# A two-layer hybrid trunk on one core: attention slots placed ahead of an evacuation, and one empty slot per eight attention units

## The chip, the cores and the metric

The kernel runs on one NeuronCore of one Trainium2 chip, in one launch. The metric is the device time of an execution in microseconds (us). All arithmetic is float32; matmul operands are cut into two float32r parts, a high and a low one, and each product is made of three matmuls.

## The reference, cut to what matters

Two groups of tokens go through the same two layers: 1024 prompt tokens and 64 sample tokens (8 sequences of 8), 1088 columns in all, with 1024 channels. The change touches layer 0 alone, whose mixer is this:

```python
proj = hn @ w_in                                  # 1024 -> 2560
a_val, a_gate, q, k, v = jnp.split(proj, [512, 1024, 1536, 2048], axis=-1)
glu = a_val * jax.nn.sigmoid(a_gate)
a = causal_depthwise_conv(concat([conv_prev, glu]), conv_w) + conv_b   # width 31
a = jax.nn.silu(layer_norm(a, ln_g, ln_b))
b = stick_breaking_attention(q, concat([k_past, k]), concat([v_past, v]), sb_bias, q_pos, k_pos)
out = concat([a, b]) @ w_out
```

The attention has 8 heads of 64 channels. For a block of 128 queries it computes

```python
z = q @ k.T * scale + bias
log_1m = where(mask, log_sigmoid(-z), 0)
after = cumsum(log_1m, reverse=True) - log_1m
wgt = exp(where(mask, log_sigmoid(z) + after, -inf))
out = wgt @ v
```

The kernel writes this with sigmoids and products: a reverse running product of sigmoid(-z) along the keys, times sigmoid(z). After the mixer each layer has a SwiGLU feed-forward network (FFN) of width 2816. k and v are outputs too, in rows of tokens, and so is the last part of the gated convolution input.

## The kernel before, in words

**Tiling.** Activations are held with channels on the partitions. The tokens are split in two groups: `GA` is columns 0 to 511, `GB` columns 512 to 1087 (512 prompt columns and the 64 sample columns), worked on as two blocks of 288. A weight tile of 1024 by 128 comes in by one DMA of 512 KB into `stage` (4 buffers, issued by SyncE's queue, L169), is split by ScalarE into its high part (L187) and by GpSimd into its low part (L189), both in `hl`. `mm3` (L238) issues the three matmuls of each product: 24 matmuls of 512 columns for a weight tile in `GA`, 48 of 288 columns in `GB`, into one `acc` tile of PSUM.

**Foreground and background.** The order of the work is the order in which the Python code issues it; each engine then takes its instructions in that order and waits on semaphores. The foreground is a row of projections. The background is a list of generators (`flow`); a call of `bg()` advances the first of them to its next `yield`. The foreground calls it at its slots: inside `block`, ahead of the third, fifth and seventh of the eight products (`slot()` at i = 2, 4, 6), and once more after the block. So a block has four slots, and a slot stands between two pieces of 12 matmuls of 288 columns in `GB`, or of 6 matmuls of 512 columns in `GA`. A generator that yields without issuing anything leaves its slot empty: TensorE then goes straight on with the next foreground piece.

**The stages of layer 0.** In this order: the input projection of `GA` (`in_proj(GA, ...)`); the input projection of `GB` (`in_proj(GB, x1, 0, bg)`), whose background is the convolution of `GA`, its layer norm, and then the attention of `GA`; the output projection and the FFN of `GA` (`run_out`, `run_ffn`), whose background is `flow_c`: the attention of `GB`, then the convolution of `GB` beside the attention of the sample tokens over the paged cache, then the layer norm of `GB`. What is left of the background is run by `drain()` when the last piece of the FFN of `GA` begins. The code as it stood before leaves the last 12 slots of that FFN with nothing to run.

**`in_proj(GB)`.** 20 blocks of 48 matmuls, in the order `EVEN`: for each of four channel groups c a value, a gate, a q and a k tile, and then four v tiles. `acc` has two buffers. After a block the code calls `flush()`, which runs what earlier blocks have put off in `post`, then `evs[i](a)`, the evacuation of this block's `acc` by VectorE (L296: times the norm factor `rr`), and then the fourth slot. What is put off in `post` is the turning of channels into output rows: for a k or v tile `rows_out` issues five TensorE transposes (four L804 into one `m` tile, one L808 into another), two ScalarE copies (L805, L809) and two DMAs (L811, L813); for a gate tile one transpose (L790), one copy and, at the end, nine DMAs. `m` is a PSUM tile with two buffers, and all transposes of the kernel go through it.

**The attention generator.** 32 units per group, (head, query block), each a chain over four engines:

- `s1(u)`: TensorE makes z from `kt`, `qa`, `qz` (L1018), ScalarE two sigmoids of z into `q` and `be` (L1023), GpSimd clears one column (L1025);
- `s2(u)`: VectorE runs two scans on `q` (L1032 on 128 columns, L1035 on the rest) and a product into `be` (L1037);
- `s3(u)`: TensorE transposes `be` in pieces of 128 into `m` (L1047), ScalarE copies them to `wt` (L1048);
- `s4(u)`: for two units at a time, TensorE multiplies by `vrow` into `o` (L1057), ScalarE copies to its place (L1060).

At each new head `operands` queues small steps for the next one: ScalarE copies (L992, L993, L997) and VectorE subtractions (L995, L998); two of them are issued per unit. `load_v` fetches `vrow` by a DMA on SyncE's queue (L1005). In `GA` a unit has 1 to 4 pieces of keys, s3 comes three units after s1, and a unit takes one slot. In `GB` it has 5 to 8 pieces, s3 comes two units after s1, and a unit takes two slots: after `s2(u - 1)` there is a `yield 1`, and s4, s3, s1 and the small steps come in the next slot. So per head s3 has eight, seven, six and five pieces in turn.

Of the kernel before, what the change touches and what calls it, by code (L numbers as in the profile page):

```python
# [46 lines left out]
GB = Grp(HALF, T, (0, 2, 288, 0))  # L47
# [10 lines left out]
def trunk_kernel(ctx, tc, x_prompt, x_sample, cache_k, cache_v, state_conformer, state_shortconv, state_pool,  # L58
# [166 lines left out]
    def w_next(live=0):  # L225
        j = wj[0]
        wj[0] += 1
        w_split(j + 3 - live)
        w_load(need(j + 6 - live))
        return hls.pop(j)  # L230
# [3 lines left out]
    def mm3(g, acc, wh, wl, x, first, last):  # L234
        for s, (w, xi) in enumerate(((wh, 0), (wh, 1), (wl, 0))):
            for b, (c0, c1) in enumerate(g.blocks):
                xs, o = (x, 0) if not isinstance(x, tuple) else (x[0], 0) if c0 < x[2] else (x[1], x[2])
                pe.matmul(acc[:, b, :c1 - c0], w, xs[:, xi, c0 - o:c1 - o],  # L238
                          start=first and s == 0, stop=last and s == 2)
# [51 lines left out]
    def norm_b(g, ps, dg):  # L291
        spread(g, ps, dg, 1.0)
# [13 lines left out]
    def flush():  # L306
        todo = post + late
        post.clear()
        late.clear()
        for f in todo:  # L310
            f()
# [4 lines left out]
    def block(g, a, h, x, ks=K0, mid=None, slot=None):  # L316
        for i, k in enumerate(ks):
            if i == 4 and mid:
                mid()
            if slot and i in (2, 4, 6):  # L320
                slot()
            mm3(g, a, h[:, 0, k], h[:, 1, k], x[k], k == ks[0], k == ks[-1])
# [344 lines left out]
    def accs():  # L667
        return accbox["p"].tile([128, len(accbox["g"].blocks), 512], F, name="acc")
# [301 lines left out]
    def attention(g):  # L970
# [3 lines left out]
        with ExitStack() as es_:  # L974
# [11 lines left out]
            def operands(h):  # L986
                hp, hh = divmod(h, 2)
                r, o = slice(hh * 64, hh * 64 + 64), slice(64 - hh * 64, 128 - hh * 64)
                k = kt_[h] = pa.tile([128, NKEY], FR, name="kt", bufs=2)
                q = qa[h] = pa.tile([128, HALF], FR, name="qa", bufs=2)  # L990
                ks, qs = kall[r, hp, 0:NKEY], qall[r, hp, g.c0:g.c0 + HALF]
                small.append(lambda: act.activation(k[r], ks, AF.Copy))  # L992
                small.append(lambda: act.activation(q[r], qs, AF.Copy))  # L993
                for c in range(0, NKEY, 512):
                    small.append(lambda c=c: dve.tensor_tensor(k[o, c:c + 512], ks[:, c:c + 512],  # L995
                                                               f32(k[r, c:c + 512]), op=OP.subtract))
                small.append(lambda: act.activation(q[o], qs, AF.Copy))  # L997
                small.append(lambda: dve.tensor_tensor(qz[hh][r], qs, f32(q[r]), op=OP.subtract))  # L998
# [28 lines left out]
            def s2(u):  # L1027
                n = 128 * (units[u][1] + 1)
                be, q = bt[u], qt.pop(u)

                e = q[:, n - 128:n][:, ::-1]
                dve.tensor_tensor_scan(e, e, ident[:, ::-1], 0.0, op0=OP.mult, op1=OP.max)  # L1032
                if n > 128:
                    e = q[:, 0:n - 128][:, ::-1]
                    dve.tensor_tensor_scan(e, e, ones[:, 0:1].to_broadcast([128, n - 128]), q[:, n - 128:n - 127],  # L1035
                                           op0=OP.mult, op1=OP.mult)
                dve.tensor_tensor(be[:, 0:n - 1], be[:, 0:n - 1], q[:, 1:n], op=OP.mult)  # L1037

            def s3(u):
                i = units[u][1]  # L1040
                be = bt.pop(u)
                w = wt[u] = pa.tile([128, i1 - u % 2, 128], F, name=f"wt{u % 2}")
                for j0 in range(0, i + 1, 4):
                    n = min(4, i + 1 - j0)
                    m = ms().rearrange("p (j n) -> p j n", j=4)
                    for j in range(n):
                        pe.transpose(m[:, j], be[:, (j0 + j) * 128:(j0 + j) * 128 + 128], ident)  # L1047
                    act.activation(w[:, j0:j0 + n], m[:, :n], AF.Copy)  # L1048

            def s4(u):  # L1050
                h, i = units[u]
                hp, hh = divmod(h, 2)
                ws = wt.pop(u - 1), wt.pop(u)
                o = op_.tile([128, 128], F, name="o2")
                for j in range(i + 2):
                    for b in range(2 if j <= i else 1):
                        pe.matmul(o[64 * b:64 * b + 64], vrow[h][:, j], ws[b][:, j], start=j == 0, stop=j == i + 1 - b)  # L1057
                for b in range(2):
                    c = (i + 1 - b) * 128
                    act.activation(qall[hh * 64:hh * 64 + 64, hp, c:c + 128], o[64 * b:64 * b + 64], AF.Copy)  # L1060
# [8 lines left out]
            for u in range(len(units) + lag + 1):  # L1069
                if 1 <= u < len(units) + 1:  # L1070
                    s2(u - 1)
                if g is GB:
                    yield 1
                if u >= lag + 2 and (u - lag) % 2 == 0:
                    s4(u - lag - 1)
                if lag <= u < len(units) + lag:
                    s3(u - lag)
                if u < len(units):
                    h, r = divmod(u, 4)
                    if r == 0 and h < 7:  # L1080
                        operands(h + 1)
                    if r == 2 and h < 7:
                        load_v(h + 1)
                    s1(u)
                for _ in range(2):
                    if small:
                        small.pop(0)()
                yield 1
# [241 lines left out]
    def in_proj(g, x, first, slot):  # L1330
        evs = [(ev_av, ev_ag, ev_q, ev_k, ev_v)[j](g, c) for j, c in EVEN]
        for i in range(first, len(evs)):
            h = w_next()
            a = accs()
            if i == first and first:
                box = {}
                block(g, a, h, x, mid=lambda: box.setdefault("d", norm_a(g, ms, D)))
                held_back = a
                continue
            elif i == first + 1 and first:  # L1340
                block(g, a, h, x)
                norm_b(g, ms, box["d"])
                evs[first](held_back)
                evs[i](a)
                for j in range(2):
                    evs[j](None, raw[j])
            else:
                rest = g is GA and i == len(evs) - 1
                block(g, a, h, x, slot=None if rest else slot)
                flush()  # L1350
                evs[i](a)
                if rest:
                    continue
            slot()

# [705 lines left out]
```

## Time and profile before

| | |
|---|---|
| median of 3 runs | 2502.1 us (2501.27 to 2504.09) |
| the profiled execution | 2503.01 us, of which the span from first to last instruction is 2501.2 us |
| TensorE (PE) busy | 2423.2 us, 97% |
| weight loads (PEld) | 2194.5 us, 88% |
| VectorE (DVE) | 1625.4 us, 65% |
| ScalarE (ACT) | 1105.2 us, 44% |
| GpSimd (POOL) | 1618.3 us, 65% |

The profile is of one execution. Busy times of matmuls are modelled and overlap, so what TensorE loses is read from its waits: the idle time before an instruction, and what ended it. "Issue" as the cause means that the profile shows no semaphore for it. A view by windows gives busy times and the granted TensorE clock (PEclk) for chosen stretches. A timeline row shows start, duration, engine, line, operation, output and inputs.

### The profile page before, as it was taken

The page shows a single profiled execution, that of the slowest core. Times are in us where ns is not written, and L with a number is a line of the kernel's source. Part 1 is how long each engine was busy: PE and PEld are TensorE (multiplying, and loading weights), DVE is VectorE, ACT ScalarE, POOL GpSimd, SP SyncE. Part 2 cuts the span into 40 slices and gives each one's busy share as a digit, 9 for nine tenths or more (in the row PEclk, how much of TensorE's full clock was granted, in tenths as well). Part 3 has the DMA queues.
Part 4 walks back from the last instruction along what each step waited for, and adds up shares of the span by engine and source line. Part 5 has one row for each costly group of instructions (what it writes and reads, how often), then busy time and mean ns, then how long its engine had stood idle before and what let it go on. Part 6 is the DMA issues. An engine that isn't in the chain of part 4 may idle for free.

```text
span 2501.2 us, 41461 instructions
## 1 busy us (share of the span) xinstructions
PE 2423.2 (97%) x15877; PEld 2194.5 (88%) x15877; DVE 1625.4 (65%) x2288; ACT 1105.2 (44%) x1877; POOL 1618.3 (65%) x1264
## 2 busy tenths in 40 slices
PE   8999999999999999999999999998999999999998
PEld 6788877788777679999999999888889988999998
DVE  3696878977777553766656533457766659666655
ACT  5535777754444343443333422244443344443333
POOL 6764334655654576788787523277888885887775
PEclk9999999999999999999999999999999999999999
DMA  7332231234565534223332311252333332233322
GB/s 225 114 110 74 76 110 51 72 103 144 175 178 174 161 91 149 68 77 91 95 93 83 119 51 43 59 148 64 92 102 102 97 98 85 85 98 115 93 85 81
DMA packets 355486, 258.32 MB, mean 103 GB/s; under 512 B 22913, under 2 KB 303617, under 8 KB 355272
## 3 DMA queue, kind: packets, MB, share of 16 engines
q1 hardware_dynamic: 355256, 255.66, 34.6%
q8 instruction: 126, 2.06, 0.3%
q14 instruction: 72, 0.59, 0.1%
q10 hardware_dynamic: 32, 0.01, 0.0%
HBM read 237.41 MB, written 18.69 MB: 102 GB/s over the span
## 4 chain that ended last, share of the span: by engine, by line
PE 72%; DVE 12%; POOL 4%; ACT 3%; issue 3%; SPq 0%; DMA 0%; DVEq 0%; ACTq 0%; POOLq 0%
PE acc L238 41%; PE acc L540 23%; POOL hl L200 2%; DVE q L1035 1%; PE o L1057 1%; DVE hb L300 1%; PE m L1159 1%; PE m L1047 1%; PE z L1182 1%; PE z L1018 1%; POOL hl L189 1%; DVE be L1037 1%; DVE sum L203 1%; DVE hid L244 1%; DVE sum L204 1%
## 5 line engine op out<-in xcount | busy, mean ns | idle before, releaser
L189 POOL TENSOR_TENSOR hl<-stage,hl 128x512 fp32r<-128x512 f32 x464 | 637.8, 1398 | 393.6 <-ACT hl L187 279.9
L238 PE MATMUL acc<-x,hl 128*128 128x512 f32 (+1 forms) x3648 | 773.2, 350 | 9.9 <-ACT hl L187 2.8
L238 PEld LDWEIGHTS acc<-x,hl 128*128 128x128 f32 x3648 | 587.4, 190 | 73.8 <-issue 5.8
L238 PE MATMUL acc<-hid,hl 128*128 128x288 f32 (+1 forms) x3096 | 545.1, 332 | 8.6 <-DVE tmp L296 4.6
L238 PEld LDWEIGHTS acc<-hid,hl 128*128 128x128 f32 x3096 | 471.0, 190 | 54.5 <-DVE tmp L296 5.1
L540 PE MATMUL acc<-x,hl 128*128 128x288 f32 (+1 forms) x2676 | 368.0, 291 | 5.8 <-POOL hl L200 3.7
L300 DVE TENSOR_TENSOR hb<-acc,hb 128x512 f32<-128x512 f32 (+1 forms) x360 | 255.6, 718 | 171.1 <-PE acc L238 169.8
L540 PEld LDWEIGHTS acc<-x,hl 128*128 128x128 f32 x2676 | 352.3, 189 | 12.0 <-POOL hl L200 7.4
L200 POOL TENSOR_TENSOR hl<-sum,hl 128x512 fp32r<-128x512 f32 x180 | 233.4, 1325 | 170.3 <-ACT hl L199 168.3
L187 ACT ACTIVATE hl<-stage 128x1024 fp32r<-128x1024 f32 x232 | 243.8, 1054 | 215.9 <-PE acc L238 149.8
L544 DVE TENSOR_TENSOR tmp<-acc,tmp 128x288 f32<-128x288 f32 (+1 forms) x420 | 174.7, 442 | 210.6 <-ACT tmp L556 106.3
L200 POOL TENSOR_TENSOR hl<-stage,hl 128x512 fp32r<-128x512 f32 x180 | 273.9, 1540 | 14.1 <-ACT hl L199 14.1
L540 PE MATMUL acc<-b,hl 128*128 128x256 f32 (+1 forms) x1548 | 217.5, 292 | 7.7 <-DVE tmp L544 5.8
L238 PE MATMUL acc<-x1t,hl 128*128 128x288 f32 x1152 | 216.3, 296 | 1.5 <-POOL hl L189 1.5
L540 PEld LDWEIGHTS acc<-b,hl 128*128 128x128 f32 x1548 | 203.3, 191 | 13.0 <-POOL hl L200 6.4
L238 PEld LDWEIGHTS acc<-x1t,hl 128*128 128x128 f32 x1152 | 195.9, 188 | 19.5 <-POOL hl L189 1.8
L199 ACT ACTIVATE hl<-sum 128x512 fp32r<-128x512 f32 x180 | 103.0, 624 | 189.6 <-DVE sum L205 169.1
L296 DVE TENSOR_TENSOR tmp<-acc,rr 128x512 f32<-128x512 f32 (+1 forms) x108 | 75.2, 710 | 135.5 <-PE acc L238 121.6
L199 ACT ACTIVATE hl<-stage 128x512 fp32r<-128x512 f32 x180 | 105.8, 619 | 69.6 <-PE acc L238 63.6
L507 POOL TENSOR_TENSOR tmp<-tmp 128x576 f32<-128x576 f32 (+1 forms) x85 | 123.6, 1454 | 9.1 <-ACT tmp L484 8.1
L244 DVE TENSOR_TENSOR hid<-tmp,hid 128x576 fp32r<-128x576 f32 (+1 forms) x66 | 78.5, 1192 | 72.0 <-ACT hid L243 72.0
L238 PE MATMUL acc<-x1a,hl 128*128 128x512 f32 x480 | 122.3, 409 | 3.0 <-POOL hl L189 1.3
(298 smaller groups left out, 3159.6 us busy)
## 6 DMA issues: line engine op xcount, KB each, us to landing
stage<-in_w_ffn_in_dram SPq DMA_DIRECT2D x176, 512.0 KB
stage<-in_w_ffn_out_dram SPq DMA_DIRECT2D x88, 512.0 KB
stage<-in_w_in_even_dram SPq DMA_DIRECT2D x40, 512.0 KB
kst<-in_cache_k_dram SPq DMA_DIRECT2D x64, 256.0 KB
vst<-in_cache_v_dram SPq DMA_DIRECT2D x56, 256.0 KB
stage<-in_w_out_even_dram SPq DMA_DIRECT2D x16, 512.0 KB
stage<-in_w_in_odd_dram SPq DMA_DIRECT2D x16, 512.0 KB
stage<-in_w_out_odd_dram SPq DMA_DIRECT2D x16, 512.0 KB
```

The costliest lines, as they stand in the source:

```text
L187: act.activation(hl[:, 0], st, AF.Copy)
L189: pool.tensor_tensor(hl[:, 1, c], st[:, c], f32(hl[:, 0, c]), op=OP.subtract)
L199: act.activation(hl[:, 0, c], x, AF.Copy)
L200: pool.tensor_tensor(hl[:, 1, c], x, f32(hl[:, 0, c]), op=OP.subtract)
L203: todo = [lambda: dve.tensor_tensor(sb, su[:, lo], su[:, hi], op=OP.add), lambda: dve.tensor_tensor(sa[:, hi], sg[:, lo], su[:, lo], op=OP ...
L238: pe.matmul(acc[:, b, :c1 - c0], w, xs[:, xi, c0 - o:c1 - o], start=first and s == 0, stop=last and s == 2)
L244: (on or dve).tensor_tensor(dst[:, 1], src, f32(dst[:, 0]), op=OP.subtract)
L296: dve.tensor_tensor(d, a, r, op=OP.mult)
L300: dve.tensor_tensor(d, a, d, op=OP.add)
L507: (dve if both and f == NF - 1 else pool).tensor_tensor(t[:, :n], t[:, :n], u[:, :n], op=OP.mult)
L540: pe.matmul(acc[:, :w2], h[:, wi, i, k], xk[:, xi], start=k == 0 and s == 0, stop=k == 3 and s == 2)
L544: dve.tensor_tensor(out, acc[:, :w2], x, op=OP.add)
```

## The change

Two edits.

- In `in_proj`, for `GB`, the block's fourth slot is taken ahead of `flush()` and `evs[i](a)` and no longer behind them. The number of slots is the same.
- In `attention`, for `GB`, every eighth unit (u = 1, 9, 17, 25, 33) yields once more between `s2(u - 1)` and the rest of the unit. So five more slots are used up, and all later background of `flow_c` comes up to five slots later; of the 12 slots without work at the end 7 are left.

```diff
@@ -1071,6 +1071,8 @@
                     s2(u - 1)
                 if g is GB:
                     yield 1
+                    if u % 8 == 1:
+                        yield 1
                 if u >= lag + 2 and (u - lag) % 2 == 0:
                     s4(u - lag - 1)
                 if lag <= u < len(units) + lag:
@@ -1347,9 +1349,11 @@
             else:
                 rest = g is GA and i == len(evs) - 1
                 block(g, a, h, x, slot=None if rest else slot)
+                if g is GB:
+                    slot()
                 flush()
                 evs[i](a)
-                if rest:
+                if rest or g is GB:
                     continue
             slot()
```

No instruction is added or removed; they change places. TensorE at the boundary between the last but one block of `in_proj(GB)` and the last, before; `tmp` is the v tile that is turned into rows, `be` the attention's weights, `z` its scores, `x` and `hl` the projection:

```order
L238 MATMUL acc<-x_7_78,hl 128x288 x6
L804 MATMUL m<-ident,tmp 128x128 x4
L808 MATMUL m<-ident,tmp 64x128
L1047 MATMUL m<-ident,be 128x128
L1018 MATMUL z_3293<-kt,qa 128x256
L1018 MATMUL z_3293<-kt,qz_2104 128x256
L238 MATMUL acc<-x_0_71,hl 128x288 x6
```

and with the change:

```order
L238 MATMUL acc<-x_7_78,hl 128x288 x6
L1047 MATMUL m<-ident,be 128x128
L1018 MATMUL z_3279<-kt,qa 128x256
L1018 MATMUL z_3279<-kt,qz_2104 128x256
L804 MATMUL m<-ident,tmp 128x128 x4
L808 MATMUL m<-ident,tmp 64x128
L238 MATMUL acc<-x_0_71,hl 128x288 x6
```

The unit's transpose and scores now come first, the five transposes for the output rows after them. ScalarE at the same boundary, before:

```order
L1023 ACTIVATE be<-z_3252,bh 128x384
L805 ACTIVATE tmp<-m 128x512
L809 ACTIVATE tmp<-m 64x128
L1048 ACTIVATE wt_3289<-m 128x128
L1023 ACTIVATE q_3296<-z_3293,bh 128x256
L1023 ACTIVATE be<-z_3293,bh 128x256
L187 ACTIVATE hl<-stage 128x1024
```

and with the change:

```order
L1023 ACTIVATE be<-z_3252,bh 128x384
L1048 ACTIVATE wt_3275<-m 128x128
L1023 ACTIVATE q_3282<-z_3279,bh 128x256
L1023 ACTIVATE be<-z_3279,bh 128x256
L805 ACTIVATE tmp<-m 128x512
L809 ACTIVATE tmp<-m 64x128
L187 ACTIVATE hl<-stage 128x1024
```

The two copies of the output rows moved behind the unit's copy and sigmoids, and still stand ahead of the split of the next weight tile. On VectorE the evacuation L296 stands behind the unit's scans in the same way, and on SyncE's queue the load of `vrow` stands ahead of the two DMAs of rows.

The second edit, on TensorE at the start of the attention of `GB`, in the first two blocks of `run_out(GA)`, before; `z_3542` are the scores of unit 0, and the next `z` are those of unit 1:

```order
L1018 MATMUL z_3542<-kt,qa 128x512
L1018 MATMUL z_3542<-kt,qz_3502 128x512
L238 MATMUL acc<-x_5_76,hl 128x512 x6
L238 MATMUL acc<-x_6_77,hl 128x512 x6
L1018 MATMUL z_3569<-kt,qa 128x448
L1018 MATMUL z_3569<-kt,qz_3502 128x448
```

and with the change:

```order
L1018 MATMUL z_3542<-kt,qa 128x512
L1018 MATMUL z_3542<-kt,qz_3502 128x512
L238 MATMUL acc<-x_5_76,hl 128x512 x6
L238 MATMUL acc<-x_6_77,hl 128x512 x6
L238 MATMUL acc<-x_7_78,hl 128x512 x6
L1018 MATMUL z_3589<-kt,qa 128x448
L1018 MATMUL z_3589<-kt,qz_3502 128x448
```

Six more matmuls of the projection stand between the two units; the same happens at units 9, 17 and 25, and after the last unit.

## The prediction

> **What bounds the kernel now.** I read the page first, then the stages by windows, then TensorE's waits in the stretches that the change touches, then the timeline at those waits.
>
> ```profile
> span 2501.2 us, 41461 instructions
> PE 2423.2 (97%) x15877; PEld 2194.5 (88%) x15877; DVE 1625.4 (65%) x2288; ACT 1105.2 (44%) x1877; POOL 1618.3 (65%) x1264
> ```
>
> TensorE is busy for 97% of the span, so a change that moves no work can win only what TensorE waits for. The average hides where that is. The next view gives busy times of each engine (with the count of instructions), then the granted clock, by stretch: the attention of `GA` inside `in_proj(GB)`, the attention of `GB` in two parts (heads 0 to 2, and heads 3 to 7 behind the seam between output projection and FFN), and the rest of the FFN of `GA`.
>
> ```profile
> core 0: us, PE busy (x) PEld busy (x) DVE busy (x) ACT busy (x) POOL busy (x), PEclk, DMA share, GB/s
> 229.50:332.30 102.80, 95.56 (x738) 86.67 (x738) 78.66 (x114) 76.86 (x174) 29.23 (x51) 0.98 0.24 66
> 344.30:411.00 66.70, 63.70 (x408) 52.67 (x408) 63.71 (x57) 53.33 (x83) 31.70 (x29) 0.97 0.27 73
> 434.20:535.00 100.80, 95.45 (x662) 78.87 (x659) 97.00 (x82) 76.71 (x121) 57.83 (x51) 1.00 0.22 63
> 545.00:938.00 393.00, 384.72 (x2076) 306.82 (x2075) 269.53 (x432) 172.83 (x334) 234.93 (x198) 1.00 0.53 157
> ```
>
> In the first row TensorE lacks 7.2 us, and VectorE (77%) and ScalarE (75%) have room. In the second and third VectorE is busy for 63.71 of 66.70 and 97.00 of 100.80 us, 96% in both, so it paces the attention of `GB`; TensorE lacks 3.0 and 5.4 us there. So the two edits meet different limits.
>
> **First edit: the slot ahead of the rows and the evacuation.** TensorE's waits from 229.5 to 332.3 (total, times, longest):
>
> ```profile
> PE m L1047 <- issue: 4.1, 5, 1.2
> PE z L1018 <- ACT qa L997: 1.8, 1, 1.8
> PE z L1018 <- ACT be L1023: 0.9, 3, 0.4
> ```
>
> The five waits of 4.1 us stand at the five block boundaries where rows of k or v are turned. The timeline of one of them:
>
> ```profile
> 317.37 0.60 PE L804 MATMUL m<-ident,tmp 128*128 128x128 f32 x4
> 317.81 0.27 PE L808 MATMUL m<-ident,tmp 128*64 128x128 f32 x1
> 318.01 0.60 ACT L805 ACTIVATE tmp<-m 128x512 f32<-128x512 f32 x1 [0.84 <-PE m L804]
> 318.70 0.30 PE L1047 MATMUL m<-ident,be 128*128 128x128 f32 x1 [0.62 <-issue]
> 319.04 0.28 ACT L1048 ACTIVATE wt<-m 128x128 f32<-128x128 f32 x1 [0.28 <-PE m L1047]
> 319.08 1.76 PE L238 MATMUL acc<-x,hl 128*128 128x288 f32 x12
> ```
>
> L804 and L808 take both `m` buffers; the unit's transpose L1047 needs one of them back, and starts 0.09 us after L805 has emptied it at 318.61. With the change the unit's transpose comes first, while both are free, and its copy L1048 of 0.28 us runs under the scores and the four L804. The second row tile then finds its buffer empty. That removes 0.62 us at three boundaries and 1.05 and 1.18 us at the other two:
>
> ```profile
> 248.58 0.30 PE L1047 MATMUL m<-ident,be 128*128 128x128 f32 x1 [1.05 <-issue]
> 294.66 0.30 PE L1047 MATMUL m<-ident,be 128*128 128x128 f32 x1 [1.18 <-issue]
> ```
>
> What is late next: at those two the scores L1018, now issued directly behind the block, need the earlier unit's sigmoid out of the single z buffer; at such places the profile already shows waits of 0.4 us (the last row of the waits above). I take 0.45 us off each of the two, and 0.6 us for the rest: 4.1 - 0.9 - 0.6 = 2.6 us. The bounds are 4.1 us (all of it) and 0, if ScalarE, in which the two copies now follow the sigmoids, hands the wait on to the next slot. Against 0 speaks the next slot's room: the copies need 0.60 + 0.26 us, and 12 matmuls of 1.76 us come before the next transpose.
>
> The same edit puts the evacuation behind the background's VectorE work, and the load of `vrow` ahead of the two row DMAs on SyncE's queue. Nobody reads those rows soon, so the DMAs cost nothing as long as the weight loads behind them run four tiles ahead. The evacuation:
>
> ```profile
> 160.98 2.34 DVE L858 SCALAR_TENSOR_TENSOR cacc<-ext,par,cacc 128x512 f32<-128x512 f32 x3
> 163.25 0.76 DVE L296 TENSOR_TENSOR tmp<-acc,rr 128x576 f32<-128x576 f32 x1
> 163.93 1.54 DVE L858 SCALAR_TENSOR_TENSOR cacc<-ext,par,cacc 128x512 f32<-128x512 f32 x2
> 156.76 12.80 PE acc L238 x96
> ```
>
> A slot of the convolution issues two steps, 1.54 us; that much later an `acc` comes free. It is wanted back a whole block later, 6.4 us (half of 12.80 us for 96 matmuls). So this costs nothing; uncovered it would be 1.54 us at each of 20 blocks. The Trainium skill, "PSUM — Partial Sum Buffer", in its closing table of what to do, says to evacuate promptly, because PSUM is tight. By that rule this edit is the wrong way round; the rows above give it a cover of 6.4 us against 1.54, and its case is the last rival.
>
> **Second edit: five empty slots.** TensorE's waits from 332.3 to 545, and the timeline of the first of them:
>
> ```profile
> PE m L1047 <- DVE be L1037: 7.6, 6, 2.7
> ...
> 349.55 1.29 DVE L300 TENSOR_TENSOR hb<-acc,hb 128x512 f32<-128x512 f32 x2
> 351.46 2.67 DVE L1035 TENSOR_TENSOR_SCAN q<-q,ones 128x768 f32<-128x768 f32 x1
> 354.24 1.90 DVE L1037 TENSOR_TENSOR be<-be,q 128x895 f32<-128x895 f32 x1
> 350.95 2.96 PE L238 MATMUL acc<-x,hl 128*128 128x512 f32 x12
> 356.29 0.95 PE L1047 MATMUL m<-ident,be 128*128 128x128 f32 x7 [2.38 <-DVE be L1037]
> 464.50 0.96 PE L1047 MATMUL m<-ident,be 128*128 128x128 f32 x7 [2.72 <-DVE be L1037]
> 508.01 0.96 PE L1047 MATMUL m<-ident,be 128*128 128x128 f32 x7 [0.65 <-DVE be L1037]
> ```
>
> The waits of over half a microsecond stand before seven pieces, that is, at the second unit of a head: VectorE has just had the longest unit and the next head's subtractions. An empty slot gives TensorE six more matmuls of 512 columns, 1.4 us (half of the row of 12 without the overlap at its end), to issue meanwhile. They fall on heads 0, 2, 4 and 6 (units 1, 9, 17, 25). VectorE's work between is the same, so its finish stays and TensorE's wait shrinks by what it has to do: 1.4 of 2.38 us in head 0, 1.4 of 2.72 in head 4, all 0.65 in head 6. In head 2 there was no wait, so nothing; the fifth slot is behind the last unit. Sum 3.4 us. The most would be four times 1.4, 5.6 us, if the lead carried over to heads 1 and 5; the least is 0, if TensorE's later scores make VectorE start later.
>
> The wait of head 0 costs more than its length. In the stretches around it and around that of head 4 (PEclk is the column of 1.00 or 0.50):
>
> ```profile
> 354.10:357.40 3.30, 1.11 (x10) 1.14 (x11) 3.16 (x3) 1.29 (x3) 3.30 (x3) 1.00 0.88 225
> 357.50:360.80 3.30, 3.30 (x10) 2.65 (x9) 3.23 (x3) 2.06 (x5) 1.60 (x3) 0.50 0.55 159
> 460.00:463.20 3.20, 1.78 (x8) 1.11 (x6) 3.09 (x4) 1.34 (x2) 0.10 (x1) 1.00 0.59 171
> 357.85 4.34 PE L238 MATMUL acc<-x,hl 128*128 128x512 f32 x12
> ```
>
> After a stretch with 1.11 us of work the clock is halved for the next, and 12 matmuls take 4.34 us and not 2.96: 1.4 us. After one with 1.78 us of work it is not. With about 1 us of wait left in head 0 this halving should go; as VectorE paces the units I count half of it, 0.7 us (bounds 0 and 1.4). The Trainium skill, "TensorE: Matmul & The Clock Gate", section on the clock gate, says that the clock falls after at least one idle window of about 3.4 us. Here it fell after a wait of 2.38 us, so that rule read literally would have no halving to win back, and the sum would be 0.7 us less.
>
> What is moved later is the rest of the background, by five slots. It has room at the end: its last piece, and the foreground behind it:
>
> ```profile
> 918.37 3.62 DVE L963 TENSOR_TENSOR hb<-hb,tmp 128x576 f32<-128x576 f32 x2
> 926.54 0.69 DVE L300 TENSOR_TENSOR hb<-acc,hb 128x512 f32<-128x512 f32 x1 [0.71 <-PE acc L238]
> 927.94 0.69 DVE L300 TENSOR_TENSOR hb<-acc,hb 128x512 f32<-128x512 f32 x1 [0.71 <-PE acc L238]
> ```
>
> A slot there takes 1.4 us (926.54 to 927.94), the background ends near 922, and by the code's count 12 slots follow; five cost 7 us of that room and no time. Without the room they would be run by `drain()` uncovered. On SyncE's queue one weight load more comes ahead of the first cache pages; they have six slots before TensorE turns them.
>
> **Sum.** 2.6 + 3.4 + 0.7 = 6.7 us. The profiled execution took 2503.01 us, so 2496.3; it lies 0.9 us above the median of the runs, 2502.1, which gives 2495.4 us.
>
> **The rivals.**
>
> *Only the first edit pays.* VectorE at 96% leaves TensorE nothing to win: lead gained at head 0 is given back as VectorE waits for the later scores. For it: 96%; against: TensorE waits for VectorE there, and not the other way. 2502.1 - 2.6 = 2499.5 us. Chance 0.18.
>
> *Nothing moves.* The row copies, now behind the sigmoids, make the next slot wait as long, and the second edit fails as above. Against it: the 1.76 us of cover. 2502.1, within a microsecond. Chance 0.08.
>
> *Slower: the sample attention falls badly against the FFN blocks.* Five slots are one block and one slot, so each later step meets the block's evacuations at another place. The waits now, from 545 to 965:
>
> ```profile
> PE m L1159 <- DVE kth L1163: 1.3, 3, 0.7
> ```
>
> There are 48 steps, of which three wait, 0.7 us at most. If each waited 0.3 us more, that is 14.4 us: 2495.4 + 14.4 = 2509.8 us. It decides from (6.7 + 5.0) / 48 = 0.24 us a step. Against it: a step takes three slots and a block four, so the steps pass through all places already. Chance 0.05.
>
> *Slower: the accumulators come free late.* If the evacuation slips by more than the block of 6.4 us, TensorE waits at every block: 20 times 1.54 us, 31 us, 2526 us after the rest of the gain. The rows show a quarter of that delay, so 0.03.
>
> **How the numbers follow.** 0.66 is left for the forecast, likeliest. A measurement of this kernel can tell about 0.2%, 5.0 us, from no change. The forecast's gain of 6.7 us has the bounds 0 to 4.1, 0 to 5.6 and 0 to 1.4, so up to 11.1 us; I give it 0.54 above 5.0 us and 0.12 below. Faster 0.54, same 0.12 + 0.18 + 0.08 = 0.38, slower 0.08. The range goes from 2490.5 (11.1 us and half a microsecond of spread) to 2501.0, which takes in the first rival and leaves out the slower ones and most of the second.
>
> **What would show it.** First edit: no L1047 wait at the row boundaries from 230 to 332 us, and L808 without one in its place. Second: L1047 before seven pieces waits about 1 us in heads 0 and 4, PEclk stays 1.00 after it, and the background ends some 7 us nearer to the last piece of the FFN. It is wrong if VectorE's share from 344 to 535 us falls while the stretch is as long, or if L1159 or L238 gains waits.

## The result and the profile after

The changed kernel is slower: a median of 2520.5 us in 6 runs (2519.28 to 2523.11) against 2501.7 us in 6 runs of the kernel before (2500.21 to 2504.09), a ratio of 1.0076 with the interval 1.0067 to 1.0086. The forecast, 2495.4 us, lies on the wrong side of no change, and so does the whole range, 2490.5 to 2501.0 us. The first lines of the profile after:

```profile
span 2519.1 us, 41449 instructions
PE 2428.4 (96%) x15877; PEld 2197.6 (87%) x15877; DVE 1619.9 (64%) x2288; ACT 1101.6 (44%) x1877; POOL 1614.9 (64%) x1264
```

The counts of instructions per engine are those of before. TensorE's share falls from 97% to 96%: it waits more. The next two views, by windows, show where. First the kernel before, by three stretches: from the start of the output projection to the first transpose of a cache page (this is the attention of `GB`; "the attention stretch" from here on), from there to the end of the FFN of `GA` ("the sample stretch"), and the rest. The columns are as in the prediction.

```profile
332.30:553.60 221.30, 209.48 (x1296) 170.32 (x1297) 187.82 (x171) 157.79 (x251) 116.75 (x104) 0.98 0.28 78
553.60:948.50 394.90, 385.74 (x2080) 307.40 (x2078) 277.14 (x440) 175.58 (x335) 238.93 (x197) 1.00 0.54 159
948.50:2501.20 1552.70, 1516.36 (x10578) 1446.38 (x10578) 936.10 (x1349) 588.14 (x966) 1088.86 (x793) 0.99 0.30 90
```

The same stretches after, with the attention of `GA` inside `in_proj(GB)` ahead of them:

```profile
229.50:328.30 98.80, 95.06 (x738) 87.52 (x738) 79.01 (x116) 77.38 (x176) 28.39 (x51) 0.97 0.25 71
328.30:573.10 244.80, 223.05 (x1326) 180.38 (x1326) 190.40 (x176) 158.28 (x253) 117.58 (x108) 0.95 0.26 73
573.10:967.50 394.40, 379.65 (x2049) 301.39 (x2047) 268.17 (x435) 171.81 (x333) 237.22 (x193) 1.00 0.53 158
967.50:2519.10 1551.60, 1514.89 (x10578) 1445.07 (x10578) 938.61 (x1349) 588.30 (x966) 1086.87 (x793) 0.99 0.30 90
```

Five empty slots bring 30 more foreground matmuls into the attention stretch (1296 to 1326) and take about as many out of the sample stretch. By the prediction's 1.4 us for six matmuls that is 7.0 us, which is no loss, and I take it off the one and add it to the other here and in every experiment below (TensorE's busy time in the sample stretch falls by 6.1 us, 385.74 to 379.65, so up to 0.9 us of a loss there may come from this round price):

- `in_proj(GB)`: 102.8 to 98.8 us, 4.0 us won;
- attention stretch: 244.8 - 7.0 = 237.8 for 221.3 us, 16.5 us lost;
- sample stretch: 394.4 + 7.0 = 401.4 for 394.9 us, 6.5 us lost;
- the rest: 1.1 us won. Together 17.9 us, the difference of the spans.

**What was won.** TensorE's waits from 229.5 to 328.3 after the change, and one of the boundaries at which it waited before (of TensorE, the last one with rows):

```profile
PE z L1018 <- ACT qa L997: 3.4, 1, 3.4
PE z L1018 <- ACT be L1023: 0.9, 1, 0.9
```

```profile
325.44 0.27 PE L1047 MATMUL m<-ident,be 128*128 128x128 f32 x1
325.55 0.60 PE L804 MATMUL m<-ident,tmp 128*128 128x128 f32 x4
326.14 0.30 PE L808 MATMUL m<-ident,tmp 128*64 128x128 f32 x1
```

All five waits of L1047 (4.1 us) are gone, and the waits for `be` add up to 0.9 us as before. The first row is the wait at the start of this attention, 1.8 us before. TensorE comes there 0.5 us earlier, but the norm chain delivers the operands 1.1 us later: ScalarE's L997 starts at 230.34 and not at 229.22 (at 230.24 with the first edit alone). So the stage wins 4.1 us and loses 1.1 at its start; the 4.0 us come about because a wait of 0.5 us for `qz` is gone as well and TensorE's busy time is 0.5 us shorter.

**What was lost.** TensorE's waits in the attention stretch after the change:

```profile
PE m L1047 <- DVE be L1037: 10.0, 4, 4.6
PE m L1047 <- ACT wt L1048: 4.4, 2, 2.4
PE z L1018 <- ACT be L1023: 2.1, 2, 1.0
PE acc L238 <- ACT hl L187: 1.9, 1, 1.9
PE o L1057 <- ACT wt L1048: 1.6, 2, 1.4
```

Before, only the first of these was there at a length (7.6 us in six waits) beside 1.3 us for L187; all waits of the stretch grew from 13.0 to 22.9 us. The second and the fifth row are new, and the third was 0.3 us: TensorE waits for ScalarE, which is busy for 158 of 245 us. Two rows of what ScalarE itself waits for, from 328 to 590 us, before:

```profile
ACT tmp L481 <- DVE tmp L296: 6.7, 5, 2.1
ACT tmp L254 <- DVE hb L300: 6.3, 3, 5.1
```

and after:

```profile
ACT tmp L481 <- DVE tmp L296: 26.7, 5, 6.9
ACT tmp L254 <- DVE hb L300: 16.0, 5, 7.7
```

These two are the rows for the foreground's values, and both grew. L481 is not attention. It is the sigmoid of the FFN's gate, in `ev_g`, which reads what the evacuation L296 has written; L254 is the square for the norm behind the residual sum L300, in `run_out`. Both are the foreground's, and in ScalarE's queue the attention's instructions stand behind them. The timeline of the longest of these waits, in head 4 after the change (the last column is the idle time ahead of the row and what ended it):

```profile
463.82 1.38 DVE L1032 TENSOR_TENSOR_SCAN q<-q,ident 128x128 f32<-128x128 f32 x1
465.24 1.82 DVE L1035 TENSOR_TENSOR_SCAN q<-q,ones 128x768 f32<-128x768 f32 x1
467.19 1.09 DVE L1037 TENSOR_TENSOR be<-be,q 128x895 f32<-128x895 f32 x1
468.19 0.69 DVE L296 TENSOR_TENSOR tmp<-acc,rr 128x512 f32<-128x512 f32 x1
468.91 0.63 ACT L481 ACTIVATE tmp<-tmp 128x512 f32<-128x512 f32 x1 [6.92 <-DVE tmp L296]
469.57 0.55 ACT L1060 ACTIVATE hb<-o 64x128 f32<-64x128 f32 x2
470.14 1.08 ACT L1048 ACTIVATE wt<-m 128x512 f32<-128x512 f32 x2
470.80 1.03 PE L1047 MATMUL m<-ident,be 128*128 128x128 f32 x7 [1.97 <-ACT wt L1048]
471.12 0.91 ACT L1023 ACTIVATE q<-z,bh 128x768 f32<-128x768 f32 x1
472.05 0.42 DVE L1032 TENSOR_TENSOR_SCAN q<-q,ident 128x128 f32<-128x128 f32 x1 [2.45 <-ACT q L1023]
```

and the same unit before:

```profile
460.28 0.69 DVE L296 TENSOR_TENSOR tmp<-acc,rr 128x512 f32<-128x512 f32 x1
460.89 0.41 DVE L1032 TENSOR_TENSOR_SCAN q<-q,ident 128x128 f32<-128x128 f32 x1
461.34 1.82 DVE L1035 TENSOR_TENSOR_SCAN q<-q,ones 128x768 f32<-128x768 f32 x1
```

Before, VectorE does the evacuation first and then the unit's scans; after, the scans and the product first (4.3 us) and the evacuation last. ScalarE stands at L481 for 6.92 us, with the copies L1060 and L1048 and the sigmoids L1023 of the next units behind it. So TensorE lacks `m` (1.97 us), and then VectorE, which paces this stretch, lacks `q` (2.45 us). The cause of the swap is in the counting. A unit takes two slots, the scans in the first of them; a block has four slots, the fourth behind the evacuation. An even number of slots ahead keeps the scans in the second and the fourth slot, an odd number puts them into the first and the third, and what the third slot issues on VectorE stands ahead of the block's evacuation. In the changed kernel the number is odd for heads 0 and 1 (one slot) and heads 4 and 5 (three), from the second unit of the pair on, and even for the others. So the swap explains 6.92 and 6.67 of the 26.7 us, in heads 4 and 5. Another 6.32 us stand in head 3, at 447.15, where the number is even: there the evacuation, at 446.38, stands behind a unit's scans that take 1.40 and 2.64 us in place of 0.41 and 1.82. The remaining two waits, 4.35 and 2.46 us at 559.32 and 586.50, lie behind the last unit's scans.

In head 0 no L481 stands in the way yet, and the wait that the prediction meant to shorten still grew. VectorE and TensorE after (two fences):

```profile
345.01 3.44 DVE L995 TENSOR_TENSOR kt<-kall,kt 64x512 fp32r<-64x512 f32 x2
348.48 1.40 DVE L1032 TENSOR_TENSOR_SCAN q<-q,ident 128x128 f32<-128x128 f32 x1
```

```profile
354.80 0.95 PE L1047 MATMUL m<-ident,be 128*128 128x128 f32 x7 [3.53 <-DVE be L1037]
```

and GpSimd at that time, after (first fence) and before (second fence, with the subtractions):

```profile
343.65 5.95 POOL L189 TENSOR_TENSOR hl<-stage,hl 128x512 fp32r<-128x512 f32 x4 [2.55 <-ACT hl L187]
```

```profile
348.23 1.29 DVE L995 TENSOR_TENSOR kt<-kall,kt 64x512 fp32r<-64x512 f32 x2
349.85 7.42 POOL L189 TENSOR_TENSOR hl<-stage,hl 128x512 fp32r<-128x512 f32 x4 [0.86 <-ACT hl L187]
```

Before, the two subtractions L995 end before GpSimd begins its splits, and take 1.29 us; after, they run beside them and take 3.44 us. The short scan runs beside the splits in both kernels and takes 1.40 us in place of 0.67 (0.42 at 339.91, where GpSimd does nothing). The Trainium skill, "SBUF — State Buffer", section "Who interferes with whom", says that a VectorE operation on two tensors with both inputs in SBUF contends with GpSimd's reads; the rows of the subtractions agree, 1.29 against 3.44 us.

**The clock.** Of the granted clock, the records of before show three stretches at half in the attention stretch, 10.2 us; those of after five, 23.9 us. Half of the 13.7 us more is work that took twice as long: 6.8 us, which with 9.9 us of added waits makes 16.7, near the 16.5 us.

**The sample stretch** shows the same wait. ScalarE there, before and after:

```profile
ACT tmp L481 <- DVE tmp L296: 23.5, 14, 4.6
```

```profile
ACT tmp L481 <- DVE tmp L296: 45.0, 15, 5.0
```

TensorE's waits after (8.9 us in all before, 13.6 after; 0.8 us of them the `L1159` that the prediction named, in its new place L1161):

```profile
PE m L1233 <- DVE kth L1165: 4.7, 5, 1.5
```

### The profile page after: what moved, and what is told of

The parts are those of the page before. It is cut to its first block, busy times and chain, and to the rows that moved or that the text cites. A ratio compares the mean times of both kernels' runs of the same rounds, so it can differ in the third digit from the quotient of the medians.

```text
span 2519.1 us, 41449 instructions
## 1 busy us (share of the span) xinstructions
PE 2428.4 (96%) x15877; PEld 2197.6 (87%) x15877; DVE 1619.9 (64%) x2288; ACT 1101.6 (44%) x1877; POOL 1614.9 (64%) x1264
## 4 chain that ended last, share of the span: by engine, by line
PE 74%; DVE 12%; POOL 3%; ACT 3%; issue 2%; DMA 0%; SPq 0%; DVEq 0%; ACTq 0%; POOLq 0%
PE acc L238 43%; PE acc L540 23%; POOL hl L200 2%; PE o L1057 1%; DVE q L1035 1%; DVE hb L300 1%; PE z L1018 1%; PE m L1047 1%; PE z L1184 1%; PE m L1161 1%; DVE kt L995 1%; DVE sum L203 1%; DVE be L1037 1%; PE o L1256 1%; DVE sum L204 1%
## 5 line engine op out<-in xcount | busy, mean ns | idle before, releaser
L300 DVE TENSOR_TENSOR hb<-acc,hb 128x512 f32<-128x512 f32 (+1 forms) x360 | 255.3, 718 | 171.0 <-PE acc L238 169.6
L187 ACT ACTIVATE hl<-stage 128x1024 fp32r<-128x1024 f32 x232 | 243.5, 1053 | 205.7 <-PE acc L238 144.0
L540 PEld LDWEIGHTS acc<-b,hl 128*128 128x128 f32 x1548 | 201.4, 189 | 13.6 <-ACT hl L199 6.4
L296 DVE TENSOR_TENSOR tmp<-acc,rr 128x512 f32<-128x512 f32 (+1 forms) x108 | 75.1, 709 | 121.2 <-PE acc L238 112.9
L255 POOL TENSOR_TENSOR ss<-ss,tmp 128x512 f32<-128x512 f32 (+1 forms) x69 | 105.4, 1528 | 30.1 <-ACT tmp L254 19.6
```

The source lines that it names most:

```text
L187: act.activation(hl[:, 0], st, AF.Copy)
L255: pool.tensor_tensor(ss[:, g.cs], ss[:, g.cs], t[:, :g.n], op=OP.add)
L296: dve.tensor_tensor(d, a, r, op=OP.mult)
L300: dve.tensor_tensor(d, a, d, op=OP.add)
L540: pe.matmul(acc[:, :w2], h[:, wi, i, k], xk[:, xi], start=k == 0 and s == 0, stop=k == 3 and s == 2)
```

## The experiments

The theory of the order: what counts is where a unit's or a step's slots fall in the block of four, since that sets what VectorE does ahead of the evacuation and what ScalarE has queued behind L481 and L254. The rivals: a price per slot (each empty slot costs TensorE or VectorE something wherever it falls), and the first edit as the cause (the evacuation behind the background's work). Where no other diff is shown, "the first edit" is that of the change, word for word. Each ratio, with its 95% interval, is against runs of the kernel before that were made beside it (medians 2500.99 to 2501.58 us). Attention and sample stretch are of the one profiled execution, with 1.4 us a slot taken off and added, as above; before they are 221.3 and 394.9 us.

**1. The first edit alone.** The kernel before with the change to `in_proj`.

> The first edit alone. Theory (order): the loss is all in the second edit, because an odd number of empty slots puts a unit's scans ahead of the foreground's evacuation on VectorE, and ScalarE then stands in its in-order queue at the foreground's sigmoid (L481) or square (L254) with the attention's copies behind it. The first edit then keeps the 4.0 us by which the changed kernel reached the output projection earlier: 2497.7 us. Rival (late evacuation): the evacuation behind the background's work is what costs, so this kernel is slower than before, 2505 to 2520 us.

2498.39 us, ratio 0.9987 (0.9977 to 0.9997); 221.3 and 395.5 us, and the output projection begins at 328.1 for 332.3 us. The first edit keeps its gain and disturbs nothing behind it. The rival that makes it the cause falls.

**2. The second edit alone.** The kernel before with the two lines in `attention`.

> The second edit alone. Theory (order): before plus the 22.8 us that the changed kernel lost after the input projection: 2522 to 2526 us. Rival (late evacuation): near before, 2497 to 2503 us.

2521.59 us, 1.0081 (1.0064 to 1.0098), 0.4 us under what I expected; 236.0 and 403.0 us. The whole loss, in both stretches, comes with the empty slots.

**3. One empty slot at the start.** The first edit, and one slot in place of five:

```diff
-                    if u % 8 == 1:
+                    if u == 1:
                         yield 1
```

> Both edits, but a single empty slot, at unit 1, so that all later units stand shifted by one slot. Theory (order): heads 3 to 7, all within the FFN, now have their scans right ahead of the evacuation, so ScalarE's wait at L481 is as long as in the changed kernel or longer (24 to 60 us) and the time is 2510 to 2530 us. Rival (price per empty slot): one slot costs a fifth of five, 2497.7 + 16.5 / 5 = 2501 us.

2521.72 us, 1.0079 (1.0062 to 1.0096); 236.0 and 404.4 us. One slot costs as much as five. ScalarE's waits from 328 to 590 us in this kernel:

```profile
ACT tmp L481 <- DVE tmp L296: 30.2, 6, 7.0
ACT tmp L254 <- DVE hb L300: 18.9, 5, 7.7
```

They are those of the changed kernel, a little longer. So one slot ahead of everything is enough for the loss, and the later four are not needed for it. Here every unit behind unit 1 stands one slot off, in the changed kernel those of heads 0, 1, 4 and 5 alone; why the attention stretch loses no more here is open.

**4. Two empty slots in each place.** Both edits, ten slots:

```diff
                     if u % 8 == 1:
-                        yield 1
+                        for _ in range(2):
+                            yield 1
```

> Both edits, but two empty slots at each of the five units instead of one (ten in all), so the scans stay where they were beside the evacuation of an FFN block. Theory (order): ScalarE's wait at L481 for L296 falls from 24.3 us in the changed kernel back to under 8 us from 328 to 590 us, and the time is 2490 to 2503 us; the upper end if unit 12, which now comes behind the seam between output projection and FFN, keeps its wait of 4.6 us and the halved clock. Rival (price per empty slot: VectorE, 96% busy, starts later by what TensorE puts in between): ten slots cost twice as much as five, 2497.7 + 2 x 16.5 = 2531 us.

2504.84 us, 1.0015 (1.0005 to 1.0025), 1.8 us over the upper end that I had given; 222.4 and 401.2 us. With pairs the scans keep their places, L481 waits 12.6 us and not 26.7 (I had expected under 8), and the attention stretch is back within 1.1 us. Ten slots cost the attention stretch less than one does: the rival of a price per slot falls. The sample stretch, ten slots later (two and a half blocks), still loses 6.3 us.

**5. and 6. Five and four empty slots behind the attention.** The first edit, and in `flow_c`, behind `yield from attention(GB)` (4 in the other kernel):

```diff
+        for _ in range(5):
+            yield 1
```

> The first edit, and the five empty slots all behind the attention of the second group, ahead of its convolution and the sample attention. Theory (place in the block): the attention stretch is as long as with the first edit alone (221.3 us from the output projection to the first cache transpose, and 7 us of slots more), and the stretch from there to the end of the FFN loses the 6.6 us that the changed kernel lost there, because the steps meet a block's evacuation elsewhere: 2505 us. Rival (the later stretch lost only because the attention handed it a backlog): 2498.4 us, as with the first edit alone.

> As the run with five slots behind the attention, but four: a whole block. Theory (place in the block): every later step stands in its block where it stood, so nothing is lost: 2497 to 2500 us. Rival (any shift of the later work against the FFN costs): 2503 to 2505 us.

Five: 2505.64 us, 1.0016 (1.0007 to 1.0026); 221.8 and 401.3 us. Four: 2501.28 us, 0.9997 (0.9987 to 1.0006); 223.7 and 395.6 us. The sample stretch as the windows show it, five and then four slots later:

```profile
557.70:952.00 394.30, 379.67 (x2049) 301.39 (x2047) 268.08 (x435) 171.81 (x333) 237.74 (x194) 1.00 0.52 154
```

```profile
557.60:947.60 390.00, 379.56 (x2055) 302.83 (x2053) 272.56 (x436) 173.87 (x334) 235.87 (x195) 1.00 0.53 157
```

With five slots behind an undisturbed attention the sample stretch loses the same 6.4 us, and ScalarE stands at L481 for 44.9 us in it, as in the changed kernel; with four, a whole block, it loses 0.7 us, and L481 waits 31.1 us. So the loss of the sample stretch is a second one, of its own, and a shift by a whole block does without it. The wait at L481 does not measure it by itself: the ten slots of experiment 4 have 30.7 us of it in that stretch, no more than the four here, and lose 6.3 us. The median of the four-slot kernel is 1.3 us over what I expected: its attention stretch, in which nothing was edited, took 2.4 us more than in experiment 1, with a wait for L387 of 2.6 and not 1.1 us and one more stretch at half clock. Why is open.

**7. and 8. The sigmoid put off.** In the FFN the sigmoid L481 and the product behind it go to `post` and run at the next block's `flush()`; once on the changed kernel, once on the first edit alone:

```diff
             if sig:
-                s = tmp()
-                act.activation(s[:, :n], t[:, :n], AF.Sigmoid)
-                pool.tensor_tensor(t[:, :n], t[:, :n], s[:, :n], op=OP.mult)
+                def later():
+                    s = tmp()
+                    act.activation(s[:, :n], t[:, :n], AF.Sigmoid)
+                    pool.tensor_tensor(t[:, :n], t[:, :n], s[:, :n], op=OP.mult)
+                post.append(later)
```

> The changed kernel, with the FFN's sigmoid L481 and the product behind it put off to the next flush, a block later, so that ScalarE no longer meets it before the evacuation L296 is done. Theory (ScalarE's in-order queue): the waits of TensorE for ScalarE in heads 4 and 5 (4.4 us at L1047, 2.1 us at L1018) and the halved clock behind them (two times 6.8 us, worth 6.8 us) go, the wait of 4.6 us in head 3 stays: 2507 to 2514 us. Rival (VectorE's backlog alone holds TensorE): 2518 to 2522 us.

> Control for the put-off sigmoid: the first edit alone, with L481 put off in the same way. Both theories: there the evacuation stands ahead of the scans and L481 waits little, so 2496 to 2500 us, as with the first edit alone.

On the changed kernel: 2507.23 us, 1.0019 (1.0009 to 1.0028); the two stretches, without the 7.0 us taken off and added:

```profile
329.20:566.10 236.90, 219.32 (x1325) 178.43 (x1326) 191.44 (x176) 158.74 (x253) 119.21 (x108) 0.96 0.27 76
566.10:953.90 387.80, 378.38 (x2049) 301.68 (x2048) 269.65 (x435) 172.24 (x333) 237.01 (x193) 1.00 0.54 160
```

that is 229.9 and 394.8 us. On the first edit alone: 2498.74 us, 0.9989 (0.9979 to 0.9998), as without it. With the background in the same slots, and only the sigmoid and its product a block later, the whole loss of the sample stretch is gone, and 7.9 of the 16.5 us of the attention stretch. By the medians, the five slots cost 22.1 us with the sigmoid in its place (2520.5 against 2498.4) and 8.5 us with it put off (2507.2 against 2498.7), so 13.6 us go with L481. The profiled execution of the control is a short one (2496.54 us), with stretches of 219.1 and 395.2 us; against that one the put-off leaves 10.8 us in the attention stretch and gives back 5.7. Of the 8.6 us the trace shows ScalarE's wait at L254, 16.0 us as in the changed kernel, since it was not put off; the wait in head 0 (3.53 us); and one of 4.60 us in head 3, where the change moves unit 12, with its long scans, behind the seam between output projection and FFN (4.61 us in the changed kernel). How they share it was not tried.

**9., 10. and 11. Whole blocks of empty slots.** The first edit, and four slots ahead of unit 17, where before the wait of 2.72 us was; then four at units 1 and 17 each; then four at 17 with the sigmoid put off:

```diff
+                    if u == 17:
+                        for _ in range(4):
+                            yield 1
```

> The first edit, and four empty slots (a whole block) at unit 17 alone, behind the seam between output projection and FFN and ahead of the longest wait that the first edit alone leaves (2.76 us in head 4, with a halved clock behind it). Theory (order): every scan stands beside its block's evacuation where it stood, ScalarE's wait at L481 from 328 to 590 us stays under 13 us, the wait in head 4 goes: 2494 to 2498 us. Rival (price per empty slot): four fifths of 16.5 us more than the first edit alone, 2511 us.

> As the run with four empty slots at unit 17, and four more at unit 1. Theory (order, and the seam): the wait of 2.3 us in head 0 goes too, but unit 12 with its long scans comes behind the seam, as with ten empty slots, and TensorE waits 3 to 5 us in head 3: 2495 to 2501 us. Rival (price per empty slot): 2498.4 + 8 x 3.3 = 2525 us.

> The first edit, four empty slots at unit 17, and the sigmoid L481 put off by a block. Theory (order): as without the put-off, and what ScalarE still loses at L481 goes too: 2493 to 2497 us, under both kernels. Rival (VectorE at 96% paces the attention whatever ScalarE does): 2498 to 2500 us, as with the first edit and the put-off sigmoid alone.

Four at 17: 2496.73 us, 0.9981 (0.9972 to 0.9991); 220.8 and 395.9 us; the wait of head 4 is gone.

Four at 1 and 17: 2499.75 us, 0.9990 (0.9981 to 0.9999); 222.0 and 397.6 us; the wait of head 0 falls to 0.89 us, but waits of 2.26 and 3.10 us come in at 402.15 and 442.42, and the sample stretch loses 2.7 us though it stands two whole blocks later. Four at 17 with the sigmoid put off: 2497.66 us, 0.9980 (0.9971 to 0.9989); 220.1 and 395.1 us, 0.7 us over what I expected, just under the rival's 2498, and the same as without putting off. Shifted by whole blocks, empty slots take away or shorten the wait at which they are aimed, as the prediction had meant them to, and four at 17 beats both kernels. But of the 2.72 us only half a microsecond shows in the stretch: TensorE waits 1.80 us in head 6, at 509.41, where it was 0.65 with the first edit alone, and 2.6 us for L387 where it was 1.1. The interval overlaps that of the first edit alone, so it is not shown that the four slots add anything to that edit's gain.

**12. Odd shifts late, with the sigmoid put off.** The first edit, L481 put off as in experiment 7, and one empty slot at each of units 17, 25 and 33, all behind the seam.

> The changed kernel with the put-off sigmoid, and without the empty slots at units 1 and 9: heads 0 to 3 stand as before, and the three empty slots at units 17, 25 and 33 are left. Theory (what the put-off sigmoid did not win back, 8.6 us from the output projection to the first cache transpose, lies in heads 0 to 3: the square L254 behind the evacuation L300, and unit 12 behind the seam): 2496 to 2500 us. Rival (an odd shift loses by VectorE alone, in the FFN too): 2503 to 2507 us.

2500.84 us, 1.0002 (0.9992 to 1.0011), 0.8 us over what I expected; 221.2 and 397.7 us. With L481 out of the way, the odd shift in heads 4 and 5 costs the attention nothing (6 and 7 stand two slots later, an even number), so the 8.6 us that experiment 7 left come with the slots at units 1 and 9 and lie in heads 0 to 3, where L254 and the seam are. The 2.8 us in the sample stretch, with waits of 2.33 and 1.81 us at 582.93 and 614.41, are open.

## Why the prediction was wrong, step by step

**The first edit** (2.6 us, bounds 0 to 4.1): the mechanism was right. 4.0 us came in the stage, just under the upper bound; the 0.45 us that I left at two boundaries for the scores and the 0.6 us for the rest were covered, and the later start of this attention, 1.1 us, was not in the sum. Alone, by its ratio, the edit is worth 0.13%, 0.03 to 0.23, about 3.3 us with 0.8 and 5.8 as bounds, so for the whole kernel 2.6 us was a fair size. That the late evacuation costs nothing there held: TensorE waits for no `acc` from 150 to 328.3 us. The rule of the Trainium skill, "PSUM — Partial Sum Buffer", to evacuate promptly did not bite at this place. It bit in the FFN, and by another way than PSUM: not the accumulator was missed, but the value that ScalarE was to read.

**The second edit** (3.4 us won, bounds 0 to 5.6). The step that failed is "VectorE's work between is the same, so its finish stays". I counted what VectorE has to do and not in which order against the foreground's evacuation, and I priced only TensorE's side; ScalarE's queue stood in the sum at nothing. Two things were missing. First, ScalarE's queue: an empty slot moves all units behind it by one place against the block, so the evacuation L296 fell behind 4.3 us of scans and product, and L481 held up the copies and sigmoids of the next units. Putting L481 off gives back 7.9 us here, and 13.6 of 22.1 us in the whole kernel (experiment 7). Second, durations are not fixed: in head 0 the two subtractions took 3.44 and not 1.29 us where they now run beside GpSimd's splits, so VectorE finished later and the wait went from 2.38 to 3.53 us where I had written 1.0. Nor did the lower bound "0" hold, since it was reasoned from TensorE's lead alone. What the remaining 8.6 us of the attention stretch are made of is known by place, heads 0 to 3, and not by cause. A sign of the kind that the prediction set did come: VectorE's share of the attention stretch fell, from 85 to 78%, and the stretch grew longer.

**The clock** (0.7 us won): the halving at head 0 did not go, as its wait did not, and others came: 6.8 us lost. The mechanism, waits that cost more than their length, was right and worked against the change. The reading that 1.11 us of work in a window halves the clock and 1.78 does not is no rule: before, a window with 1.72 us was followed by the halved clock too (last section).

**The shift of the later background** (no cost): the step that failed is "a step takes three slots and a block four, so the steps pass through all places already". They do, but over the whole stretch it still matters where they begin: 5 slots lost 6.4 to 6.5 us (experiment 5 and the changed kernel), 10 lost 6.3, 8 lost 2.7 and 4 lost 0.7 to 1.0. With L481 put off 5 lost nothing, but 3 lost 2.8. That the loss of five slots goes through L481 is shown by experiment 7; why a beginning off by one costs when the steps go round, and what the ten, eight and three slots lose by, is open. The room at the end of the FFN was there as predicted: the last stretch took no longer.

**The rivals.** The sample attention falling badly, priced at 14.4 us, was right in place and in sign; the loss was 6.5 us, under half of that, and TensorE's waits for it stand on other lines than L1159. The larger loss, in the attention stretch, is in no rival, because each of them asked who waits for VectorE or TensorE and none who stands in ScalarE's queue. With 0.08 the slower side had far too little: the order of L296 and the scans could be read from the order of the instructions, and the 6.7 and 6.3 us that ScalarE already waited were in the trace of before.

## What to carry to other kernels

When background work with a period runs in the slots of a foreground with a period of its own, an empty slot is a shift against that period: insert whole blocks, or an amount that keeps the background's long work off the slot ahead of the evacuation. Before costing such a shift, write down for each in-order engine which foreground instruction it will stand at and what of the background is queued behind that, also on the engines that are not busy. And take a duration from a row in which the same neighbours were running.

## What the runs showed of the hardware

The clock fell to half also after a wait shorter than the stretch by which it changes (1.97 us, ahead of the row at 470.80). The changed kernel's records, by windows around two falls and one place without:

```profile
441.50:444.90 3.40, 0.00 (x0) 0.00 (x0) 3.27 (x3) 0.00 (x0) 3.40 (x4) 1.00 0.81 211
445.00:448.30 3.30, 3.30 (x13) 3.18 (x14) 3.27 (x4) 1.15 (x2) 1.35 (x2) 0.50 0.48 153
468.80:472.20 3.40, 1.06 (x8) 0.73 (x7) 0.92 (x3) 3.23 (x7) 1.26 (x1) 1.00 0.00 0
472.30:479.00 6.70, 6.14 (x16) 4.88 (x16) 5.39 (x6) 4.95 (x8) 4.47 (x5) 0.50 0.02 4
```

```profile
523.50:526.80 3.30, 1.62 (x10) 1.08 (x9) 3.20 (x3) 0.78 (x2) 0.10 (x1) 1.00 0.50 159
526.90:530.20 3.30, 3.30 (x20) 2.84 (x18) 3.23 (x4) 3.06 (x5) 0.10 (x1) 1.00 0.03 7
```

and in the kernel before:

```profile
415.50:418.80 3.30, 1.72 (x7) 0.76 (x5) 3.16 (x4) 3.30 (x5) 1.13 (x2) 1.00 0.00 0
418.90:422.20 3.30, 3.00 (x7) 2.44 (x8) 3.29 (x3) 0.35 (x1) 3.30 (x3) 0.50 0.00 0
```

The changes lie on multiples of about 3.41 us from one another (445.0 and 472.3 are eight apart). In the changed kernel the clock was halved after windows with 0.00 and 1.06 us of TensorE work, and not after one with 1.62 in 3.30; in the kernel before it was halved after one with 1.72. So these modelled busy times give no limit that tells the two outcomes apart. The Trainium skill, "TensorE: Matmul & The Clock Gate", gives at least one idle window of about 3.4 us as the condition; the windows here were up to half busy and the clock fell all the same, so the measurement decides. Since the windows lie at fixed distances, whether a wait of 2 to 3 us costs a halving may depend on where it falls in them, and this may be why one kernel's runs differ by a tenth of a per cent. In experiment 1 they are 2494.82 to 2497.86 us at a mean granted clock of 0.995 and 2498.74 to 2500.15 at 0.992; the others, 2496.59 to 2499.52 us, lie at 0.993 and 0.994. It was not tried by itself.
